# All transfers of a two-layer transformer kernel in the order of emission, with stores a little behind what they store

## The chip, the cores and the metric

The kernel runs on one core of one Trainium2 chip. The metric is the device time of one execution in microseconds. Before the change it is 3485.12 us, the median of three runs (3480.47, 3485.12 and 3489.89).

A core has engines with an instruction queue each: TensorE (PE, matrix products), VectorE (DVE), ScalarE (ACT), GpSimd (POOL) and SyncE (SP). In this kernel SP does nothing but issue transfers, and it issues all of them.

## What is computed

A transformer with two layers works on 1024 latent tokens (a grid of 16 x 64) and 256 context tokens, 1024 features each, all in fp32. Layer 0 mixes tokens with neighbourhood attention (16 heads, a window of 8 x 16, a bias by relative position, and the whole context), layer 1 with grouped-query attention (16 query heads, 4 key heads, root-mean-square norm of queries and keys, rotary positions). A SwiGLU FFN (hidden size 2816) follows each mixer. Shift, scale and gate of every norm are modulations made from a condition vector by the weights `ada_w`. Cut from the reference:

```python
for i in range(2):
    mod_l = (silu(c) @ ada_w[i] + ada_b[i]);  mod_c = (silu(c_ctx) @ ada_w[i] + ada_b[i])
    sh1, sc1, g1, sh2, sc2, g2 = split(mod)          # for latents (l) and context (c) apart
    a_l, a_c = ada_norm(h, norm_mix[i], sh1_l, sc1_l), ada_norm(hc, norm_mix[i], sh1_c, sc1_c)
    y_l, y_c = neighbourhood_attention(...) if i == 0 else qknorm_gqa(...)
    h = h + g1_l * y_l
    h = h + g2_l * swiglu_ffn(ada_norm(h, norm_ffn[i], sh2_l, sc2_l), ffn_w_in[i], ffn_w_out[i])
    if i == 0: ...                                   # the same for hc
return rms_norm(h, norm_final)

# neighbourhood attention, of one query row
p = softmax(concat([q @ k_window * scale + bias (masked), q @ k_context * scale]))
o = p[..., :n] @ v_window + p[..., n:] @ v_context
```

## The kernel before

**Numbers.** Every product is made from three: each fp32 operand is split in a high and a low part, and the kernel adds high x high, high x low and low x high. So most tiles exist twice (`qh` and `ql`, `wh` and `wl`, `ah` and `al`).

**Stages.** A startup makes the first norm and the first projections. Then comes the attention of layer 0 in two passes over its query tiles. A unit is 128 queries of one head, a pair is two units. Pass A has 48 pairs (16 heads, three pairs each), pass B 32 (16 heads, two each). Pass A runs beside the projections of queries, keys and values of the heads that come later, pass B beside the output projection. Then the FFN of layer 0, the projections that layer 1 starts with, its attention (64 pairs), its FFN and the last norm.

**One pair.** Scores `S` and `X` from keys `K` and queries `Qs` (PE), bias and maximum (DVE), exponentials and sums `Pt` (ACT), `Pt` scaled by the reciprocal sum `rc` (POOL, L803), transposed by PE (`T`, L810), split into high and low (`pT`, ACT L818 and DVE L823), multiplied with the values (`o`, L492), copied by ACT (`ob`, L832), the high and low columns added by POOL (`r`, L838). Of two heads that share 128 features, the second one's pair gets a tile `z`: two transfers of 64 x 256 put rows of the one head's `r` and of the other's into it (`z<-r`; the rows 0-63 and 64-127 change places), POOL adds the rest (L850, L851), and a transfer stores it (`Od<-z` in layer 0, `O1d<-z` in layer 1).

**Through DRAM.** Queries and keys go to scratch in DRAM, from where each head loads `Qs`, `K` and `Vt`. A block's projection ends in `finish_qk0` (layer 0; ACT makes `qh` at L755, DVE `ql` at L757) or `finish_qk1` (layer 1), and `stack_out` stores `qh` and `ql` as two transfers of 2x64x512, 2x64x256 for the context block: `dst[:, 0:64, c0:c0 + n]` has the two heads of a pair as its first dimension. `finish_v0` stores values (`Vd<-vt`), `out_add0` the updated residual (`H0d<-xr`). The weights of the modulation are loaded in pieces `adaw` and summed on DVE (`adaj`, L487).

**What sets the order.** The stages of all pairs are issued by `Plan` in the order of a written-out table, which gives each stage a place within a period (`PERIODA = 7622`, `PERIODB = 5560`, `PERIOD1 = 8172` ns). Between them `Plan` opens slots for the background: `Lanes` (`bg`) holds the projections, weight splits, norms and modulation as generators and advances them by one instruction per slot of an engine. `bg.now` is the plan's clock: it counts table time (and 650 ns per `tick` outside of the table), not device time. `bg.sleep(ns)` makes a generator yield until the plan's clock has moved on; it puts no instruction anywhere.

From the attention of layer 0 to the end of the program one context sets which engines issue in the order of emission:

```python
top.enter_context(tc.manual_schedule(engines={ET.PE, ET.Activation, ET.DVE, ET.Pool}))
```

SP isn't in it, so the order of the transfers in SP's queue is chosen by the framework's scheduler when the program is built. On the chip SP takes them in that order. In the startup SP is in the set already.

Of the kernel before, what the change touches and what calls it, by code (L numbers as in the profile page):

```python
# [31 lines left out]
# columns of the packed vector array  # L32
# [40 lines left out]
def _build(tc, nc, I, O, top):  # L73
# [28 lines left out]
    silc = const.tile([P, 16], F32, name="silc")        # silu(c) | silu(c_ctx) as columns  # L102
# [33 lines left out]
    def norm(tag, src, there, n, tmp, bank, done, direct=0, line=0):  # L136
        """the reciprocal root mean square of a block, from its chunks as they come, then the steps done(rs); the squares
        of the last direct ones go to the tensor engine one by one"""
# [52 lines left out]
    def apply_norm(tag, src, rs, G, sh, ah, al, tmp):  # L191
        """the norm's gain and shift, split into hi and lo"""
# [21 lines left out]
    # DRAM scratch  # L214
# [23 lines left out]
    def exp_ln_tables(after):  # L238
        """the one table set that serves both Exp and Ln, once the last Silu is through"""
        with tc.issue_after(after.ins):  # L240
            s.preload_act_table_set("natural_log_exp_and_others")
# [3 lines left out]
    # ================= layer 0: modulation, first norm =================  # L245
    acts = [None] * 3

    # relative-position bias laid out per (head, query, key tile offset, key)
# [13 lines left out]
    def startup():  # L262
        """the norm of every block and the first projections, issued in the order of emission"""
        ET = mybir.EngineType
        with ExitStack() as ph:
# [69 lines left out]
            # silu(c) as rows on every partition  # L335
# [52 lines left out]
            def modulation(m):  # L388
                """shift on the vector engine, scale on the tensor engine"""
# [17 lines left out]
            def apply0(kc):  # L407
                """a chunk of the first block, already scaled by 1/rms"""
# [23 lines left out]
            def first_qk(b):  # L432
                """keys and queries of the first pair, chunk by chunk in turn"""
# [60 lines left out]
    class Ring:  # L494
        """places used in turn: one is free when what had it before was given back"""
# [18 lines left out]
    class Temps:  # L514
        """fixed tiles by name, each in use until it is given back"""
# [16 lines left out]
    class Job:  # L532
        """weight units and the generator of the products with them, which may start when the first need are there"""
# [5 lines left out]
    class Lanes:  # L539
        """work in the background of an attention, or on its own, for engines that issue in the order of emission: the  # L540
        products advance by cost, what comes before and after a group of them by one instruction per slot of its
        engine, and only when the step before it should be through"""
# [4 lines left out]
        def __init__(self, third):  # L547
            # weights: two places, and a third one as long as its pool is there
            self.third, self.wx = third, None
            self.rings = dict(w=Ring(3), x=Ring(2))  # L550
            self.lo, self.cap = "GD", 6.0       # engines of the weights' low parts, most credit
            self.main, self.credit, self.now = [], 0.0, 0.0
            self.lines = [], [], []             # by urgency
            self.busy = dict(A=0.0, D=0.0, G=0.0)   # until when an engine takes nothing
            self.enter("weights", self.weights(), 0.0, 1)
# [5 lines left out]
        def follow(self, job, gen):  # L561
            """later products with the same weights"""
            job.heir = self.add(job.tag, [], gen)
            return job.heir
# [15 lines left out]

        def sleep(self, ns):
# [4 lines left out]
        def slot(self, engine):  # L586
            for it in self.side:
# [10 lines left out]
        def place(self, kind):  # L598
            """a weight unit's tiles"""
# [10 lines left out]
        def weights(self):  # L610
            """the units of the next jobs in turn, each loaded and split into hi and lo"""
# [53 lines left out]
        def tick(self, cost=1.0):  # L665
            """a slot of every engine, outside the attention's table"""
# [74 lines left out]
    QCOL = (0, 768, 512)         # columns of the queries of each block: the first pass of the attention takes two  # L741
# [19 lines left out]
    # One attention unit is 128 queries of one head, a pair of them 256. Its stages are issued in the order of a  # L761
    # table that repeats for every pair, with slots between them for the background work.
# [5 lines left out]
    class Pair:  # L768
        """two units; the context's keys (part 0, of both units in one bank) and the other parts"""
        def __init__(self, h, b, wid, blocks):  # L770
            self.h, self.b, self.nm = h, b, None
# [62 lines left out]
        def r(self):  # L834
            """sum of the hi and lo columns; of the second head of two, the rows 0-63 and 64-127 change places"""
# [4 lines left out]
            if self.h % 2 == 1:  # L840
                self.z_ = pb.tile([P, 256], F32, name="z", bufs=2)
                self.r0, self.r1 = rr[0, self.b], r
                dma(out=self.z_[0:64, :], in_=self.r0[64:128, :])
                dma(out=self.z_[64:128, :], in_=self.r1[0:64, :])

        def z(self):
            """both rows summed into the two heads' 128 features"""
            if self.h % 2 == 1:
                z = self.z_
                g.tensor_tensor(z[0:64, :], z[0:64, :], self.r0[0:64, :], ALU.add)  # L850
                g.tensor_tensor(z[64:128, :], z[64:128, :], self.r1[64:128, :], ALU.add)  # L851
                dma(out=self.out[self.h // 2][:, self.b * P:(self.b + 2) * P], in_=z[:])
                self.written.add((self.h // 2, self.b))

    class Plan:
        """the stages of all pairs in the order of their tables"""
# [3 lines left out]
        def __init__(self, phases):  # L860
            """of each phase: period, table, pairs, background products per slot, time until the next"""
# [27 lines left out]
    class Halves:  # L889
        """a block's 8 chunks in two tiles"""  # L890
# [7 lines left out]
    class Ffn:  # L898
        """what is left of a layer's output projection, that of block 1, and the FFN. The norms of the other blocks run
        behind the projection, that of block 1 behind the first products of the others"""  # L900
        def __init__(self, layer, blks, last, resid, g1, g2):
# [15 lines left out]
            if layer == 0:  # L917
                bg.add(tag, out(NJ - 4), lambda job: self.mm2(job, NJ - 4, whole), dst="x")
                # the last products of the context first
# [5 lines left out]
            # the last products of block 0 before those of block 1  # L925
# [14 lines left out]
        def start(self, h, tmp, hp, wx, psp, pool, norm):  # L940
            """with what the attention left; norm(b) gives gain and shift"""
# [70 lines left out]
        def silu(self, j, b, ps, k):  # L1012
# [6 lines left out]
            last = s.activation(sa[:, :n], ps[:, :n], AF.Silu)  # L1019
            self.rings["a"].give(k)  # L1020
            self.gates[j, b] = sa, i
            if (j, b) == (NJ - 1, 1):
                exp_ln_tables(last)
# [846 lines left out]
```

## Time and profile before

| what | us |
|---|---|
| median of three runs | 3485.12 |
| lowest and highest run | 3480.47, 3489.89 |
| span of the profiled execution | 3479.7 |
| PE busy | 3157.8 (91%) |
| DVE, ACT, POOL busy | 1951.5, 1362.9, 1008.5 |
| bytes moved | 363.41 MB, 194855 packets |

The profiled execution has no time of its own beside its span of 3479.7 us. The granted clock of PE over it is 0.957 of full speed. In the stages: the startup ends at about 170 us, pass A at about 790, pass B at about 990; the FFN of layer 0 goes to 2000, the preparation of layer 1 to 2100, its attention to 2690, and its FFN and the end to 3480.

In rows of the profile, L12 is a line of the kernel, `out<-in` names the tiles, and x is a count of instructions. In a view of waits a row reads: engine, instruction, what it waited for, us in total, times, the longest. SPq is SP's queue, with the time that each issue took. In a view of windows PE, PEld (weight loads), DVE, ACT and POOL have their busy time, then come the granted clock, the mean busy share of the 16 DMA engines and GB/s.

### The profile page before, as it was taken

To read this page: it belongs to the slowest core of one execution; us is meant where nothing else is said; L and a number is where in the kernel's file an instruction comes from. 1 tells how busy PE (TensorE), PEld (TensorE's weight loads), DVE (VectorE), ACT (ScalarE), POOL (GpSimd) and SP (SyncE) were. 2 spreads that over 40 slices of the span, in tenths; PEclk is the share of its full clock that TensorE was granted. 3 is DMA by queue.
4 is the path that set the end of the run, shared out by engine and by line. 5 is a ranking of instruction groups with operands and counts; after the bars stand their busy time and mean duration, and the time that the engine had idled before them with its cause. 6 is when DMAs were issued, how large, how long until landed. Compare 5 with 4: busy or idle time off the path is not lost.

```text
span 3479.7 us, 48144 instructions
## 1 busy us (share of the span) xinstructions
PE 3157.8 (91%) x17352; PEld 2706.9 (78%) x17352; DVE 1951.5 (56%) x4147; ACT 1362.9 (39%) x3305; POOL 1008.5 (29%) x959
## 2 busy tenths in 40 slices
PE   6767786868999999999999978999999999999998
PEld 4657685757877888888888767888888788888887
DVE  6347454556767655333333747898897534334335
ACT  3224342446753111111111437898887421121123
POOL 3224343445752000000000414666654200000002
PEclk8878898988999999999999989999999999999999
DMA  6546454556853343111111242333332211111111
GB/s 225 133 146 193 147 165 138 161 178 193 249 175 122 115 132 104 37 37 37 37 37 43 104 129 82 100 93 96 100 100 72 88 55 49 43 55 49 43 55 61
DMA packets 194855, 363.41 MB, mean 104 GB/s; under 512 B 30393, under 2 KB 94265, under 8 KB 192569
## 3 DMA queue, kind: packets, MB, share of 16 engines
q1 hardware_dynamic: 194616, 360.33, 32.8%
q8 instruction: 138, 2.26, 0.3%
q14 instruction: 101, 0.82, 0.1%
HBM read 283.71 MB, written 70.64 MB: 102 GB/s over the span
## 4 chain that ended last, share of the span: by engine, by line
PE 60%; DVE 4%; DMA 3%; ACT 1%; POOL 1%; issue 1%; DVEq 0%; ACTq 0%; POOLq 0%; SPq 0%
PE pg L714 5%; PE pa L714 5%; PE pg L713 5%; PE pg L715 5%; PE pa L715 5%; PE pa L713 5%; PE pm L1056 5%; PE pm L1057 5%; PE pm L1055 5%; PE T L810 3%; PE o L492 3%; PE S L1543 1%; PE S L1544 1%; PE ps L713 1%; PE ps L715 1%; PE ps L714 1%
## 5 line engine op out<-in xcount | busy, mean ns | idle before, releaser
L634 POOL TENSOR_TENSOR wl<-wr,wh 128x512 fp32r<-128x512 f32 x119 | 158.6, 1334 | 1443.6 <-ACT wh L632 1436.0
L803 POOL TENSOR_SCALAR Pt<-Pt,rc 128x1280 f32<-128x1280 f32 (+3 forms) x288 | 298.4, 1036 | 495.7 <-DVE rc L798 208.1
L810 PE MATMUL T<-ident,Pt 128*128 128x128 f32 x1952 | 312.9, 281 | 141.2 <-POOL Pt L803 136.5
L818 ACT CAST pT<-T 128x256 fp32r<-128x256 f32 (+2 forms) x672 | 305.1, 477 | 234.9 <-PE T L810 230.7
L810 PEld LDWEIGHTS T<-ident,Pt 128*128 128x128 f32 x1952 | 241.9, 144 | 198.7 <-POOL Pt L803 148.6
L823 DVE TENSOR_TENSOR pT<-T,pT 128x256 fp32r<-128x256 f32 (+2 forms) x672 | 342.2, 535 | 43.1 <-ACT pT L818 42.6
L632 ACT CAST wh<-wr 128x512 fp32r<-128x512 f32 x334 | 207.7, 623 | 343.3 <-PE pg L714 158.6
L714 PE MATMUL pa<-al,wh 128*128 128x512 f32 (+1 forms) x880 | 325.3, 370 | 6.1 <-POOL al L132 4.8
L1055 PE MATMUL pm<-hh,woh 128*128 128x512 f32 (+1 forms) x912 | 330.4, 362 | 0.0
L1056 PE MATMUL pm<-hl,woh 128*128 128x512 f32 (+1 forms) x912 | 329.4, 361 | 0.0
L1057 PE MATMUL pm<-hh,wol 128*128 128x512 f32 (+1 forms) x912 | 329.3, 361 | 0.0
L1067 DVE SCALAR_TENSOR_TENSOR h<-pm,modB,h 128x512 f32<-128x512 f32 (+1 forms) x368 | 242.4, 662 | 150.3 <-PE pm L1057 150.3
L1019 ACT ACTIVATE sa<-pa 128x512 f32<-128x512 f32 (+1 forms) x110 | 60.9, 554 | 676.6 <-PE pa L715 676.5
L713 PE MATMUL ps<-ah,wh 128*128 128x512 f32 (+1 forms) x688 | 273.4, 397 | 57.7 <-DVE ql L757 20.2
L713 PE MATMUL pa<-ah,wh 128*128 128x512 f32 (+1 forms) x880 | 324.2, 368 | 1.2 <-ACT ah L197 1.2
L713 PE MATMUL pg<-ah,wh 128*128 128x512 f32 (+1 forms) x880 | 325.1, 369 | 0.0
L715 PE MATMUL pa<-ah,wl 128*128 128x512 f32 (+1 forms) x880 | 324.5, 369 | 0.1
L714 PE MATMUL pg<-al,wh 128*128 128x512 f32 (+1 forms) x880 | 324.2, 368 | 0.0
L715 PE MATMUL pg<-ah,wl 128*128 128x512 f32 (+1 forms) x880 | 323.7, 368 | 0.0
L492 PE MATMUL o<-pT,Vt 128*128 128x256 f32 x1952 | 298.9, 292 | 9.6 <-DVE rc L797 8.6
L1031 DVE TENSOR_TENSOR sa<-sa,pg 128x512 f32<-128x512 f32 (+1 forms) x110 | 69.8, 634 | 392.1 <-PE pg L715 392.1
L634 DVE TENSOR_TENSOR wl<-wr,wh 128x512 fp32r<-128x512 f32 x215 | 170.2, 792 | 206.0 <-ACT wh L632 205.7
(260 smaller groups left out, 7397.5 us busy)
## 6 DMA issues: line engine op xcount, KB each, us to landing
wr<-in_fin SPq DMA_DIRECT2D x88, 512.0 KB
adaw<-in_adaT SPq DMA_DIRECT2D x160, 256.0 KB
wr<-in_wqkv SPq DMA_DIRECT2D x53, 512.0 KB
wr<-in_fout SPq DMA_DIRECT2D x44, 512.0 KB
wr<-in_wo SPq DMA_DIRECT2D x32, 512.0 KB
z<-r SPq DMA_DIRECT2D x144, 64.0 KB
aw<-in_ada0n SPq DMA_DIRECT2D x8, 1024.0 KB
Qs<-Q1d SPq DMA_DIRECT2D x32, 256.0 KB
```

The lines of the kernel that those rows point to most:

```text
L492: t.matmul(o_ap, lhsT=u.V[:, kb, :], rhs=u.pT[:, i, :], start=i == 0, stop=i == len(u.blocks) - 1)
L634: (g if self.engine == "G" else v).tensor_tensor(lo[:, c], raw[:, c], hi[:, c].bitcast(F32), ALU.subtract)
L713: t.matmul(ps, lhsT=hi[:, c], rhs=ah[:, kc, :n], start=kc == 0, stop=False)
L714: t.matmul(ps, lhsT=hi[:, c], rhs=al[:, kc, :n], start=False, stop=False)
L715: t.matmul(ps, lhsT=lo[:, c], rhs=ah[:, kc, :n], start=False, stop=kc == KC - 1)
L803: g.tensor_scalar(Pt, Pt, u.rc[:, 2:3], 1.0, ALU.mult, ALU.mult)
L810: t.transpose(T[:, i * P:(i + 1) * P], u.Pt[:, (i0 + i) * P:(i0 + i + 1) * P], ident[:])
L818: s.copy(u.pT[:, i0:i0 + n, :P], u.T[c])
L823: v.tensor_tensor(u.pT[:, i0:i0 + n, P:], u.T[c], u.pT[:, i0:i0 + n, :P].bitcast(F32), ALU.subtract)
L1055: t.matmul(ps[:, :n], lhsT=hi[:, c], rhs=hh[:, cols], start=i == 0, stop=False)
L1056: t.matmul(ps[:, :n], lhsT=hi[:, c], rhs=hl[:, cols], start=False, stop=False)
L1057: t.matmul(ps[:, :n], lhsT=lo[:, c], rhs=hh[:, cols], start=False, stop=i == 1)
```

## The change

SP joins the engines that issue in the order of emission, and some stores and exchanges are emitted later by the plan's clock than what makes them. For this `Lanes` gets a list of calls that are due at a time of the plan's clock: `later` enters one, and every slot first makes those that are due. Comments and docstrings are removed, which is not shown.

```diff
-        top.enter_context(tc.manual_schedule(engines={ET.PE, ET.Activation, ET.DVE, ET.Pool}))
+        top.enter_context(tc.manual_schedule(engines={ET.PE, ET.Activation, ET.DVE, ET.Pool, ET.SP}))
...
     class Lanes:
+        count = itertools.count()
...
+            self.due = []
...
+        def later(self, ns, fn):
+            heapq.heappush(self.due, (self.now + ns, next(self.count), fn))
+
+        def flush(self, end=None):
+            while self.due and (end is None or self.due[0][0] <= end):
+                heapq.heappop(self.due)[2]()
...
         def slot(self, engine):
+            self.flush(self.now)
...
     class Pair:
         def r(self):
...
                 self.r0, self.r1 = rr[0, self.b], r
+                bg.later(1600, self.swap)
+
+        def swap(self):
+            if not self.swapped:
+                self.swapped = True
                 dma(out=self.z_[0:64, :], in_=self.r0[64:128, :])
                 dma(out=self.z_[64:128, :], in_=self.r1[0:64, :])
+
+        def store(self):
+            dma(out=self.out[self.h // 2][:, self.b * P:(self.b + 2) * P], in_=self.z_[:])
+            self.written.add((self.h // 2, self.b))
 
         def z(self):
             if self.h % 2 == 1:
+                self.swap()
                 z = self.z_
                 g.tensor_tensor(z[0:64, :], z[0:64, :], self.r0[0:64, :], ALU.add)
                 g.tensor_tensor(z[64:128, :], z[64:128, :], self.r1[64:128, :], ALU.add)
-                dma(out=self.out[self.h // 2][:, self.b * P:(self.b + 2) * P], in_=z[:])
-                self.written.add((self.h // 2, self.b))
+                bg.later(2200, self.store)
...
         def finish_qk0(ps, dst, scale, b):
...
             banks["free"] += 1
+            yield from bg.sleep(1300)
             stack_out(dst, hi[:, :n], lo[:, :n], BLK[b][0] if scale is None else QCOL[b], n)
...
         # finish_v0 and out_add0, ahead of their stores
+            yield from bg.sleep(1300)
...
     # finish_qk1
-        tp.give(xn, qh, ql)
+        tp.give(xn)
+        yield from bg.sleep(1300)
         stack_out(dst, hi[:, :n], lo[:, :n], c0, n)
+        tp.give(qh, ql)
...
     # at the last Silu of an FFN: the next table set is loaded without a tie to that instruction
-                exp_ln_tables(last)
+                exp_ln_tables(None)
```

The listings below are rows of SP's queue, in its order: first the program before, then the changed one. The number in a name tells the instances of a tile apart; an instance may have another number in the other program.

The first place is in pass A, near its beginning, where the queries of the third pair of heads are stored (`Qd2_94<-qh`, `ql`) and weights of the modulation are loaded. Before:

```order
L81 DMA adaw_1505<-in_adaT0 128x512
L81 DMA Qd2_94<-qh_1540 2x64x512
L81 DMA Vt_1647<-Vd0_108 128x640
L81 DMA wr_1558<-in_wqkv0 128x1024
L81 DMA Qd2_94<-ql_1541 2x64x512
L81 DMA Qd2_94<-qh_1600 2x64x256
L81 DMA Vt_1647<-Vd0_108 128x256
L81 DMA braw_1650<-Bd_91 128x384
L81 DMA Qd2_94<-ql_1601 2x64x256
L81 DMA adaw_1531<-in_adaT0 128x512
```

And now:

```order
L81 DMA adaw_1505<-in_adaT0 128x512
L81 DMA adaw_1531<-in_adaT0 128x512
L81 DMA wr_1558<-in_wqkv0 128x1024
L81 DMA Qd2_94<-qh_1540 2x64x512
L81 DMA Qd2_94<-ql_1541 2x64x512
L81 DMA adaw_1619<-in_adaT0 128x512
L81 DMA Qd2_94<-qh_1600 2x64x256
L81 DMA Qd2_94<-ql_1601 2x64x256
L81 DMA Vt_1647<-Vd0_108 128x640
L81 DMA Vt_1647<-Vd0_108 128x256
L81 DMA braw_1650<-Bd_91 128x384
```

Stores of `qh` and `ql` stand directly behind each other, the two `adaw` loads that stood on both sides of these stores stand ahead of them, and the loads of the values (`Vt_1647`) come behind them all.

The second place is also in pass A, at the exchanges of `z_3379` and `z_3482` and the stores of the keys `Kd4_104`. Before:

```order
L81 DMA z_3379<-r_3377 64x256
L81 DMA Kd4_104<-qh_3396 2x64x512
L81 DMA wr_3412<-in_wqkv0 128x1024
L81 DMA Od2_114<-z_3379 128x256
L81 DMA Kd4_104<-ql_3397 2x64x512
L81 DMA Qs_3632<-Qd3_95 128x768
L81 DMA z_3621<-r_3268 64x256
L81 DMA K1_3633<-Kd3_103 128x640
L81 DMA z_3482<-r_3480 64x256
L81 DMA adaw_3588<-in_adaT0 128x512
L81 DMA K2_3634<-Kd3_103 64x640
L81 DMA Kd4_104<-qh_3504 2x64x512
```

And now:

```order
L81 DMA z_3379<-r_3035 64x256
L81 DMA z_3379<-r_3377 64x256
L81 DMA wr_3412<-in_wqkv0 128x1024
L81 DMA Kd4_104<-qh_3394 2x64x512
L81 DMA Kd4_104<-ql_3395 2x64x512
L81 DMA Od2_114<-z_3379 128x256
L81 DMA adaw_3453<-in_adaT0 128x512
L81 DMA Vt_3488<-Vd1_109 128x640
L81 DMA Vt_3488<-Vd1_109 128x256
L81 DMA braw_3491<-Bd_91 128x384
L81 DMA z_3482<-r_3133 64x256
L81 DMA z_3482<-r_3480 64x256
```

The two halves of a `z` now stand together, the store `Od2_114<-z_3379` comes behind both key stores instead of between them, and the next head's loads (`Qs_3632`, `K1_3633`), which stood among these stores, come after this piece.

The third place is in the attention of layer 1, where the keys and values of the third of the four key heads are loaded (`K1`, `K2` and `Vt`, 128x1280 each in all). Before:

```order
L81 DMA o32_21356<-O1d0_136 128x512
L81 DMA K1_20436<-K1d1_134 128x1280
L81 DMA Qs_19664<-Q1d2_127 128x512
L81 DMA K2_20437<-K1d1_134 64x1280 x2
L81 DMA z_19863<-r_19604 64x256
L81 DMA Q1d3_128<-ph_19700 2x64x512
L81 DMA z_19726<-r_19724 64x256
L81 DMA Vt_20441<-V1d_135 128x1280
L81 DMA Q1d3_128<-pl_19701 2x64x512
L81 DMA O1d1_137<-z_19726 128x256
L81 DMA Qs_19930<-Q1d3_128 128x512
L81 DMA z_19863<-r_19861 64x256
```

And now:

```order
L81 DMA z_20259<-r_20257 64x256
L81 DMA wr_20318<-in_wqkv1 128x1024
L81 DMA O1d2_138<-z_20259 128x256
L81 DMA z_20388<-r_20134 64x256
L81 DMA z_20388<-r_20386 64x256
L81 DMA K1_20450<-K1d1_134 128x1280
L81 DMA K2_20451<-K1d1_134 64x1280 x2
L81 DMA Vt_20455<-V1d_135 128x1280
L81 DMA Qs_20457<-Q1d4_129 128x512
L81 DMA Q1d5_130<-ph_20359 2x64x512
L81 DMA Q1d5_130<-pl_20360 2x64x512
L81 DMA O1d2_138<-z_20388 128x256
```

The loads of the group were spread between exchanges and stores of a pair of heads (`z_19726`) that lies well ahead of the group's use; now they stand together, behind the exchange of `z_20388`, a pair that comes later in the program.

More of the change, by code (lines that the diff above doesn't have):

```diff
@@ L238, in exp_ln_tables @@
     def exp_ln_tables(after):
-        with tc.issue_after(after.ins):
+        with tc.issue_after(after.ins) if after else ExitStack():
             s.preload_act_table_set("natural_log_exp_and_others")
@@ L770, in __init__ @@
         def __init__(self, h, b, wid, blocks):
-            self.h, self.b, self.nm = h, b, None
+            self.h, self.b, self.nm, self.swapped = h, b, None, False
             self.u = [Unit(), Unit()]
@@ L1018, in silu @@
             sa = self.tmp.tile([P, 512], F32, name="sa", bufs=2)
-            last = s.activation(sa[:, :n], ps[:, :n], AF.Silu)
+            s.activation(sa[:, :n], ps[:, :n], AF.Silu)
             self.rings["a"].give(k)
@@ L1487, in finish_qk1 @@
         e.tensor_tensor(lo[:, :n], x[:, :n], hi[:, :n].bitcast(F32), ALU.subtract)
-        tp.give(xn, qh, ql)
+        tp.give(xn)
+        yield from bg.sleep(1300)
         stack_out(dst, hi[:, :n], lo[:, :n], c0, n)
+        tp.give(qh, ql)
     heads1 = {}
```

## The prediction

> **What bounds the kernel now.** First the span, then the busy time by stages (window in us; its length; busy time of each engine with its instructions; granted clock, DMA share, GB/s).
>
> ```profile
> span 3479.7 us, 48144 instructions
> ```
> ```profile
> 170.00:790.00 620.00, 447.67 (x2737) 403.79 (x2736) 328.69 (x942) 228.25 (x670) 231.96 (x262) 0.86 0.51 160
> 790.00:990.00 200.00, 181.91 (x1226) 165.16 (x1225) 140.59 (x484) 137.50 (x418) 134.79 (x157) 0.96 0.72 212
> 990.00:2000.00 1010.00, 993.33 (x5135) 849.26 (x5134) 503.14 (x871) 222.03 (x405) 147.47 (x115) 0.99 0.24 79
> 2000.00:2100.00 100.00, 77.67 (x396) 62.51 (x395) 47.16 (x87) 43.61 (x97) 17.55 (x13) 0.90 0.42 123
> 2100.00:2690.00 590.00, 571.53 (x3781) 499.93 (x3779) 506.05 (x1160) 497.57 (x1305) 350.36 (x312) 0.99 0.31 92
> 2690.00:3480.00 790.00, 773.06 (x3473) 639.18 (x3471) 338.42 (x473) 181.99 (x315) 72.99 (x55) 0.99 0.17 56
> ```
>
> The first number behind each length is PE. The two FFNs (rows three and six) are PE with 17 us idle each: nothing that transfers do is worth much there. The first pass of the layer-0 attention (170 to 790, "pass A") has 620 - 447.67 = 172 us without PE, more than half of what the kernel has, at a clock of 0.86. Pass B has 18, the preparation of layer 1 (2000 to 2100) 22, its attention 18. Whatever this change does is decided in pass A. Its waits (who waits for whom; us, times, longest):
>
> ```profile
> POOL z L851 <- DMA z<-r: 119.3, 20, 20.3
> DVE adaj L487 <- DMA adaw<-in_adaT: 75.3, 12, 17.0
> PE T L810 <- POOL Pt L803: 133.4, 30, 16.2
> DVE ql L757 <- DMA Kd<-ql: 25.6, 6, 9.7
> DVE ql L757 <- DMA Qd<-ql: 25.6, 4, 11.0
> PE ps L713 <- DVE ql L757: 20.2, 5, 8.5
> ```
>
> PE waits for the scaled probabilities Pt; POOL, which makes them, stands in order behind a z that waits for its halves to be exchanged, and DVE, which makes their scale, behind an adaj that waits for weights. So the roots are transfers, and these are issued by SP alone. What SP's queue waits for in the same window, the two largest:
>
> ```profile
> SPq L81 <- POOL z L851: 58.7, 18, 8.4
> SPq L81 <- DMA Kd<-ql: 48.3, 15, 4.8
> ```
>
> One such place, by the timelines of SP and POOL and a window:
>
> ```profile
> 263.54 0.56 SPq L81 DMA_DIRECT2D Kd<-qh  x1
> 272.62 0.33 SPq L81 DMA_DIRECT2D Od<-z  x1
> 273.05 0.49 SPq L81 DMA_DIRECT2D Kd<-ql  x1
> ```
> ```profile
> 271.62 0.98 POOL L851 TENSOR_TENSOR z<-z,r 64x256 f32<-64x256 f32 x1 [10.03 <-DMA z<-r]
> ```
> ```profile
> 265.00:275.00 10.00, 1.13 (x6) 1.13 (x7) 3.57 (x7) 0.35 (x2) 3.29 (x3) 0.55 0.21 65
> ```
>
> The store Od<-z is the next in SP's order and waits nine us for POOL's z, with a ready Kd<-ql and loads behind it, while PE does 1.13 us of work in ten and the transfers run at a share of 0.21. That is the loss the change can give back.
>
> **What order can't give back.** The stores of queries and keys (2x64x512) are narrow. A stretch in which they run alone, one of wide loads in the startup, the count of what pass A moves, and two issues:
>
> ```profile
> 170.00:174.00 4.00, 4.00 (x20) 3.30 (x19) 0.00 (x0) 0.60 (x1) 0.00 (x0) 1.00 0.13 51
> 10.00:20.00 10.00, 6.47 (x43) 3.91 (x42) 8.74 (x17) 5.63 (x12) 2.53 (x2) 0.84 1.00 416
> ```
> ```profile
> q1 hardware_dynamic: 61334, 98.86, 50.3%
> Kd<-qh SPq DMA_DIRECT2D x14, 256.0 KB
> Kd<-ql SPq DMA_DIRECT2D x14, 256.0 KB
> Qd<-qh SPq DMA_DIRECT2D x11, 256.0 KB
> Qd<-ql SPq DMA_DIRECT2D x11, 256.0 KB
> Qd<-ql SPq DMA_DIRECT2D x7, 128.0 KB
> Kd<-qh SPq DMA_DIRECT2D x7, 128.0 KB
> Kd<-ql SPq DMA_DIRECT2D x7, 128.0 KB
> Qd<-qh SPq DMA_DIRECT2D x6, 128.0 KB
> ```
> ```profile
> 164.53 4.74 SPq L81 DMA_DIRECT2D Qd<-qh  x1
> 169.37 4.95 SPq L81 DMA_DIRECT2D Qd<-ql  x1
> ```
>
> A share of 0.13 is two engines of sixteen, at 51 GB/s; 256 KB (0.262 MB) take 5.1 us, and SP's own issues back up behind them at the same pace (4.74 and 4.95 us instead of half a us). Pass A has 50 of 256 KB and 27 of 128 KB, 16.6 MB, or 326 us. The other 98.86 - 16.6 = 82.2 MB at 416 GB/s would take 198 us, in which these two engines carry their part too. Together 524 us, so of pass A's 620 at most 96 can go by any order of the same transfers. The Trainium skill, in "DMA: Bandwidth & Descriptors", section "Rules for kernel authors", has the same: an outermost dimension below 16 confines a transfer to that many engines. The rows agree (0.13 for two), and by that rule alone nothing is gained here: rival (a).
>
> **The change part by part.** No instruction is removed or added that costs time: the same DMAs are issued by the same queue, and the delays are of the plan's clock, which only picks the place in the order. The listing has two POOL instructions less and two DVE ones more (about a us each, by the row of z above), which is below any term. What moves:
>
> Pass A, stores and exchanges behind what makes them. Od<-z now comes 2200 ns of the plan later, so SP should no longer stand for POOL's z, 58.7 us in 18 waits. At the place above the transfers had almost drained; where narrow stores are still draining, SP's wait costs nothing. Half, -29. Both halves of z now stand together behind r; by the listing of the transfers, of the 24 exchanges 12 had narrow stores among the six transfers ahead of the second half, and now 4 have: that eases the 119.3 us of POOL, but the queue's bound is the same, so it is in that half. The weights adaw move up by 6 to 18 places to where they are emitted. DVE's longest wait for them, 17.0, and PE's longest for Pt, 16.2, are of one size; I take one of these as gone, -15, since the other eleven are in the same queue.
>
> Against it: qh and ql now leave together. By the listing, of 82 narrow stores of layer 0 28 stood directly behind another, now 45. A load behind a pair lands after 10.3 us instead of 5.1, unless it was early enough. Two such on PE's path, +10. The 1300 ns also hold the tiles qh and ql longer; DVE waits for these 51.2 us in 10 waits already, of which PE feels 20.2. Each longer by 1.3 x (620 of the trace against 48 pairs x 7.622 = 366 of the plan) = 2.2 us, 22 in all, of which PE feels 20.2/51.2: +9. Pass A: -29 - 15 + 10 + 9 = **-25**. Bounds: -96 by the engines' work; above, if each of the 17 new pairs is felt, 17 x 5.1 = 87, with the 9 and less the 44 saved: +52.
>
> Pass B and the loads of a head. These were hoisted by the scheduler and now leave where they are emitted.
>
> ```profile
> PE S L1270 <- DMA K<-Kd: 6.5, 8, 2.0
> PE S L1269 <- DMA K<-Kd: 4.4, 1, 4.4
> ```
>
> They are already just in time: 10.9 us of PE over 16 heads. By the plan, the last K stands 8.6 us ahead of its use instead of 10.4; 1.8 us at each head would be +29. But the loads no longer wait behind stores that wait for z, which would give back up to the 10.9. I take **+3**, near the row of 10.9, as the queue runs at 0.72 and has room.
>
> Layer 1, preparation. These links of the chain of waits are stores that the next load needs:
>
> ```profile
> 2059.87 11.25 DMA K1d<-ph
> 2071.84 17.63 DMA K1d<-ph
> ```
>
> Each of some four stores in a row leaves 1.3 us later, +5; the stores of h (2 MB, 5 us at 416 GB/s) now stand among those of V1d; the second group's loads, hoisted into this stretch, leave it, -5 or so. **+3**, between -10 and +15.
>
> Layer 1, attention. Keys and values of a group come 12.5 us of the plan ahead of use instead of 68.
>
> ```profile
> L81 SPq DMA_DIRECT2D K<-K1d x18: 320/468/1693, 2167.8 to 2531.1; - x18
> ```
>
> Three issues a group, so six groups. K1, K2 and Vt of a group are 1.97 MB, at pass B's 212 GB/s 9.3 us: hidden by 3 us, and not if a narrow pair (10.3) is ahead. **+1**, from -8 (its PE idle is 18) to 6 x (9.3 + 10.3 - 12.5) = +43. FFNs, startup, tail: the same order or PE-bound, 0.
>
> Sum -25 + 3 + 3 + 1 = -18 on the profiled 3479.7, 3461.7. The median run, 3485.1, lies 5.4 above that execution, so **3467 us**, 0.5% faster.
>
> **Rivals.** (a) Pass A is bound by its narrow stores, and order moves the wait from z and adaw to whatever is behind them. For it: 326 us on two engines, and PE's clock and idle time don't depend on which wait is named. Against: the share of 0.21 at 265 to 275. Gains of 20 against +9, +10 and +7: within 5 us of 3485. (b) The loads' head start is what hid the narrow stores. A load that is hoisted past a qh and ql pair lands in time; in order of emission it stands behind it. It decides from the point where 10.3 us exceed the lead: pass B's 8.6 is below that, layer 1's 12.5 just above. 16 heads x 1.8 = +29, and half of the layer-1 bound, +21, less 25 give +25: 3510; with pass A's gain gone as well 3535. The skill's section "Queues, rings and completion order" in the same page has each engine take descriptors in the order of its ring, which is what makes a load wait there; the 4.74 us issue agrees. (c) The stalls on POOL and DVE go altogether. Pairs finish at
>
> ```profile
> L832 ACT COPY ob<-o x48: 579/587/592, 208.7 to 772.6; 128x512 f32<-128x512 f32 x48
> L832 ACT COPY ob<-o x6: 586/587/592, 285.0 to 326.7; 128x512 f32<-128x512 f32 x6
> ```
>
> 12.0 us each over pass A (563.9 / 47), and 8.3 in a quiet stretch (41.7 / 5), where there are few narrow stores. At that pace 47 x 3.7 = 172 would go; the two engines stop it at 96: 3485 - 70 to 3485 - 96, about 3400. (d) The scheduler's order was near that of emission, and nothing changes: not so in pass A, where the listing of SP differs in most rows, but true of the FFNs.
>
> **Chances.** My forecast 0.45 (3450 to 3476), (a) and (d) 0.22, (b) 0.22, (c) 0.11. 0.3% is 10.5 us, about the spread of the three runs (3480.47 to 3489.89), and what can be told from no change. Faster by over that: 0.43 of the forecast's and (c)'s 0.11, with 0.01 of (a): 0.55. Within: the rest of (a) and (d) and 0.01 of the forecast, 0.22. Slower: (b) and 0.01 of the forecast, 0.23. The range leaves out half of (b) and half of (c): 3410 to 3510. The forecast's own range is 3450 to 3476.
>
> **What would show it.** Right: in pass A SP's wait for POOL z near nothing, POOL's for z<-r below 80, DVE's for adaw below 60, PE busy 447 in about 595 instead of 620, the last ob copy at about 750. The waits for Kd<-ql and Qd<-ql on DVE grow to some 70. Pass B: PE's wait for K 10 to 20. Layer 1: no wait of PE for K<-K1d over 3 us. (a) shows the same PE idle with other names on it, (b) PE waiting for K in pass B with 2 us at each head or Vt and K at the groups, (c) pairs at 8 to 9 us throughout. I am wrong if the two-engine time isn't a floor, that is if pass A ends before 690, or if it ends later than 795.

## The result, and the profile after

The changed kernel takes 3602.72 us (median of four runs, 3599.16 to 3605.32) against 3486.1 for the kernel before in the same session: 1.0336 of it, with a 95% interval of 1.032 to 1.0353. It is 117 us slower. The forecast was 3467, and the top of the range 3510.

The span of the changed kernel, and three of its stages (length, busy PE, PEld, DVE, ACT, POOL, granted clock, DMA share, GB/s): pass A, pass B, the attention of layer 1.

```profile
span 3601.1 us, 48031 instructions
```
```profile
170.00:835.00 665.00, 449.04 (x2684) 404.60 (x2684) 316.17 (x916) 220.69 (x647) 212.28 (x248) 0.82 0.46 143
835.00:1067.00 232.00, 193.04 (x1244) 173.54 (x1243) 149.32 (x510) 144.68 (x440) 138.96 (x163) 0.91 0.67 198
2180.00:2800.00 620.00, 573.52 (x3763) 500.43 (x3762) 508.58 (x1162) 497.58 (x1308) 347.07 (x309) 0.98 0.30 88
```

In its window of pass A PE is busy about as long as before, but the window is 45 us longer, and everything beside PE is less used: the DMA share went from 0.51 to 0.46. Windows set by eye don't hold the same work, so the stages are best measured between ACT's copies `ob`, one for each pair of units: 48 in pass A, 32 in pass B, 64 in layer 1. From the starts of the first and the last copies (for pass B from pass A's last):

| stage, us | before | changed | difference |
|---|---|---|---|
| start to first copy | 208.7 | 210.0 | +1 |
| pass A, first to last copy | 563.9 | 625.0 | +61 |
| pass B | 210.0 | 231.8 | +22 |
| FFN of layer 0 and preparation of layer 1 | 1115.2 | 1113.3 | -2 |
| attention of layer 1 | 582.7 | 619.7 | +37 |
| last FFN and end | 799.3 | 801.2 | +2 |

Pass A between these copies, before and then changed:

```profile
208.70:772.60 563.90, 415.00 (x2572) 375.06 (x2571) 308.38 (x884) 214.30 (x629) 218.97 (x246) 0.87 0.51 162
210.00:835.00 625.00, 426.21 (x2573) 384.71 (x2572) 305.14 (x885) 214.72 (x629) 207.89 (x243) 0.83 0.47 146
```

PE has the same work in both, but for a product or two. Its busy time is 11 us longer, at a granted clock of 0.83 instead of 0.87, and the other 50 us are idle time (148.9 before, 198.8 now).

The waits of the engines in pass A, those that answer to the ones shown of before:

```profile
POOL z L871 <- DMA z<-r: 190.6, 20, 19.6
PE T L821 <- POOL Pt L814: 163.0, 25, 17.5
DVE adaj L487 <- DMA adaw<-in_adaT: 52.9, 11, 17.0
DVE ql L768 <- DMA Kd<-ql: 24.9, 7, 8.4
DVE ql L768 <- DMA Qd<-ql: 23.0, 3, 9.6
```

And SP's queue there:

```profile
SPq L81 <- DVE rawB L487: 89.7, 17, 10.9
SPq L81 <- POOL z L872: 30.7, 10, 4.2
SPq L81 <- DMA Kd<-ql: 28.4, 8, 4.6
```

SP's wait for POOL's z fell from 58.7 to 30.7, as the change has it. In its place stands one that was 19.5 before: SP waits 89.7 us for the products `adaj` of DVE (which write `rawB`), because the next load `adaw` goes into a tile that they still read. Behind it stands the exchange of z, and POOL's wait for it is 190.6 instead of 119.3. One such round, by the timelines of SP, POOL and PE:

```profile
305.54 0.33 SPq L81 DMA_DIRECT2D Od<-z  x1
305.96 9.72 SPq L81 DMA_DIRECT2D adaw<-in_adaT  x2
...
319.58 1.24 SPq L81 DMA_DIRECT2D z<-r  x2
```
```profile
323.20 0.71 POOL L871 TENSOR_TENSOR z<-z,r 64x256 f32<-64x256 f32 x1 [12.30 <-DMA z<-r]
```
```profile
325.35 0.69 PE L821 MATMUL T<-ident,Pt 128*128 128x128 f32 x2 [9.29 <-POOL Pt L814]
```

Two adaw loads take SP 9.7 us: the second waits for DVE. Then come the next head's loads, and then the exchange, for which POOL, and behind it PE, have been waiting. In pass B and in layer 1 SP can be seen to stand for another pair of transfers:

```profile
849.39 0.38 SPq L81 DMA_DIRECT2D Od<-z  x1
859.10 0.80 SPq L81 DMA_DIRECT2D o<-Od  x2
859.98 0.38 SPq L81 DMA_DIRECT2D Qs<-Qd  x1
860.41 1.62 SPq L81 DMA_DIRECT2D K<-Kd  x3
```
```profile
868.33 0.66 PE L1292 MATMUL S<-K,Qs 128*128 128x384 f32 x1 [9.13 <-DMA K<-Kd]
```
```profile
2463.31 6.37 SPq L81 DMA_DIRECT2D O1d<-z  x1
2478.29 0.33 SPq L81 DMA_DIRECT2D o<-O1d  x1
```
```profile
2481.91 0.62 ACT L1592 CAST ah<-o 128x512 fp32r<-128x512 f32 x1 [12.89 <-DMA o<-O1d]
```

The load `o<-Od` reads what the store `Od<-z` writes, and is now emitted right behind it. SP stands from one to the other, 9 us for a store of 128 KB with narrow ones ahead of it in the first case and 8.6 in the second, and K's loads, or ACT's next copies, are late by that. But SP's time at such places is hardly new. For `Od<-z` to land it waited 43.7 us over both passes before (150 to 1060 us) and 32.7 now, all but 0.2 of it in pass B:

```profile
SPq L81 <- DMA Od<-z: 32.5, 8, 10.2
```

For `O1d<-z` in the attention of layer 1 it was 15.2 before and is 22.4. New is what stands behind: PE's wait for K in pass B went from 10.9 to 30.1, ACT's for `o<-O1d` in layer 1 from 6.7 to 27.4. What grew most among SP's own waits in layer 1 is the one for DVE to be through with a weight tile (`wl`), from 46.1 to 124.4.

### The profile page after: what moved, and what is told of

It is laid out like the page before. It is cut to its first block, busy times and chain, and to the rows that moved or that the text cites. A ratio compares the mean times of both kernels' runs of the same rounds, so it can differ in the third digit from the quotient of the medians.

```text
span 3601.1 us, 48031 instructions
## 1 busy us (share of the span) xinstructions
PE 3186.1 (88%) x17352; PEld 2728.3 (76%) x17352; DVE 1950.3 (54%) x4149; ACT 1363.7 (38%) x3305; POOL 997.3 (28%) x957
## 4 chain that ended last, share of the span: by engine, by line
PE 57%; DVE 4%; DMA 3%; ACT 1%; POOL 1%; issue 1%; SPq 0%; DVEq 0%; ACTq 0%; POOLq 0%
PE pg L725 5%; PE pg L724 5%; PE pg L726 5%; PE pa L725 5%; PE pa L726 5%; PE pa L724 5%; PE pm L1076 5%; PE pm L1075 5%; PE pm L1077 5%; PE T L821 3%; PE o L492 3%; PE S L1568 1%; PE S L1569 1%; PE ps L724 1%; PE ps L725 1%; PE ps L726 1%
## 5 line engine op out<-in xcount | busy, mean ns | idle before, releaser
L492 PEld LDWEIGHTS o<-pT,Vt 128*128 128x128 f32 x1952 | 260.2, 193 | 33.3 <-DVE pT L834 18.0
```

Of the source, the lines that this page charges most:

```text
L492: t.matmul(o_ap, lhsT=u.V[:, kb, :], rhs=u.pT[:, i, :], start=i == 0, stop=i == len(u.blocks) - 1)
```

## The experiments

Each ratio is to the kernel before on the same chip. Stage times are from the copies, as in the table.

### The order, or the delays?

The change does two things, and each was done alone. The first run takes SP out of the manual order again; the second leaves SP in it and has none of the delays. Both load the table set behind the last Silu without a tie, as the change does; the first shows that this costs nothing.

```diff
 # first run: the changed kernel
-top.enter_context(tc.manual_schedule(engines={ET.PE, ET.Activation, ET.DVE, ET.Pool, ET.SP}))
+top.enter_context(tc.manual_schedule(engines={ET.PE, ET.Activation, ET.DVE, ET.Pool}))
 # second run: the kernel before
-top.enter_context(tc.manual_schedule(engines={ET.PE, ET.Activation, ET.DVE, ET.Pool}))
+top.enter_context(tc.manual_schedule(engines={ET.PE, ET.Activation, ET.DVE, ET.Pool, ET.SP}))
-                exp_ln_tables(last)
+                exp_ln_tables(None)
```

> The changed kernel with SP's queue again in the scheduler's order: only the delays (and the small moves on the engines that they bring) are left. Theory O (the order of SP's queue costs the 121 us: in order of emission SP stands for instructions that aren't through yet, and what is queued behind it is late): 3475 to 3500. Theory D (the delays cost it: every store and exchange leaves later, and the loads that need them too): 3570 to 3610.

> The kernel before with SP in the order of emission and no delay; PE, DVE, ACT and POOL have the same order as before, instruction by instruction (the one tie of the last table load is gone, as in the change). Theory O: slower than the change, since SP now also stands for each z and each qh right behind its emission: 3620 to 3700. Theory D: near 3485.

The delays alone: 3481.69 us, ratio 0.9991 (0.9981 to 1.0), pass A 564.7, pass B 209.9, layer 1 579.9. They cost nothing and gain next to nothing, as long as the scheduler places the transfers. The order alone: 3590.33, ratio 1.0302 (1.0285 to 1.0319), pass A 595.5, pass B 238.8, layer 1 621.5. Since the other engines' orders are the same there, row for row, the whole of these 107 us is SP's order. That it would be slower than the change with its delays was wrong: it is 12 us faster. The delays cost 30 us more in pass A once the order is that of emission, and give 7 back in pass B. With the order alone POOL's wait for z<-r in pass A is 119.4 us, as long as before, and SP's for the tiles of adaw is 83.2: the longer wait for the exchange goes with the delays, and the other 32 us of pass A are lost without it.

### The narrow stores

The prediction had the narrow stores as the floor of pass A. So they were made wide, in the kernel before and in the changed one: each half of `stack_out` becomes two transfers with 64 rows as their first dimension.

```diff
-        dma(out=dst[:, 0:64, c0:c0 + n], in_=tmp_hi)
-        dma(out=dst[:, 64:128, c0:c0 + n], in_=tmp_lo)
+        for r, x in ((0, tmp_hi), (64, tmp_lo)):
+            for i in range(2):
+                dma(out=dst[i, r:r + 64, c0:c0 + n], in_=x[i * 64:i * 64 + 64])
```

> The kernel before, each 2x64xn store of queries and keys split into two of 64xn, so that the outermost dimension has 64 rows; nothing else. Theory N (narrow stores on two engines are what makes pass A long): their 326 us go to about 40, and pass A's 620 us come down by 60 to 130; 3355 to 3430. Against it (the two engines are only busy while everything waits for something else): 3470 to 3490.

> The changed kernel with the same split of the stores. If the order of emission costs only because a late load stands behind a narrow pair (10.3 us), the cost of 117 us over the kernel before mostly goes: within 25 us of the run with the split alone. If it costs because SP stands in order for things that aren't ready, it stays: 70 to 120 us above that run.

The kernel before with wide stores: 3227.84 us, ratio 0.9264 (0.925 to 0.9278). That is 255 us, or 7.4%, far more than expected, and the fastest kernel of this study. The first copy comes at 157.4 instead of 208.7, pass A takes 403.1 instead of 563.9, pass B 190.2 instead of 210.0, layer 1 570.8 instead of 582.7. Its window of pass A, and four of its stores with their size and the median us to landing:

```profile
170.00:560.00 390.00, 368.22 (x2502) 334.59 (x2501) 308.75 (x854) 205.76 (x609) 219.64 (x243) 1.00 0.75 226
```
```profile
Kd<-qh SPq DMA_DIRECT2D x24, 128.0 KB, 3.7
Kd<-ql SPq DMA_DIRECT2D x24, 128.0 KB, 2.9
Qd<-qh SPq DMA_DIRECT2D x20, 128.0 KB, 2.8
Qd<-ql SPq DMA_DIRECT2D x20, 128.0 KB, 2.5
```

PE is busy 368 of 390 us at full clock, and the share is 0.75 where it was 0.51: the stores no longer have two engines to themselves while the others are idle.

The changed kernel with wide stores: 3360.95, ratio 0.9644 (0.9626 to 0.9661). It is 133 us behind the other, more than the 117 without. So narrow stores are not why the order of emission costs. Its pass A takes 499.2, 96 us more than the other's, and pass B 220.4, 30 more. The same two waits stand in it (SP's, and POOL's; from 165 to 760 us, so with the first part of pass B):

```profile
SPq L81 <- DVE rawB L487: 84.5, 18, 12.0
```
```profile
POOL z L872 <- DMA z<-r: 128.1, 22, 15.5
```

In the kernel before with wide stores these are 17.6 and 21.3. Only in layer 1 was part of the loss due to the narrow stores: it is 11 us there (581.6 against 570.8) instead of 37.

### Place by place

Now each place at which SP was seen to stand was moved in the changed kernel, one at a time: the adaw loads 4000 ns of the plan later, and their products with them; the loads of the heads' results only 5000 ns after their store; the exchange at once.

```diff
 # adaw: its load, as go(), no longer at its place
+                    clock.later(4000, go)
 # the results
-            self.written.add((self.h // 2, self.b))
+            bg.later(5000, lambda: self.written.add((self.h // 2, self.b)))
 # and out_add0 stores the residual without its sleep(1300)
 # the exchange
-                bg.later(1600, self.swap)
+                self.swap()
```

> The changed kernel, with each load of modulation weights (adaw) emitted 4000 ns of the plan after its place, so that DVE should be through with the tile's last contents when SP comes to it. Theory Q (in order of emission the head of SP's queue stands on a transfer that can't start, here a load into a tile that DVE still reads, and the exchange of z behind it comes late): SP's wait for DVE rawB in pass A falls from 90 us below 30, pass A from 625 (first to last of its 48 ob copies) to 575 to 600, the time to 3555 to 3580. Rival (SP waits there only because it is ahead of the others; the wait is harmless): 3590 to 3610, pass A 615 to 630.

> The changed kernel, with the loads of the heads' results (o<-Od, o<-O1d) allowed only 5000 ns of the plan after the store that they read, instead of right behind it; the store of the residual goes out without its delay, since it would otherwise stand behind a load that waits for it. Theory Q: SP no longer stands for Od<-z and O1d<-z to land; pass B from 232 to 210 to 222, the attention of layer 1 from 620 to 590 to 605, the time 3555 to 3580. Rival (pass B and layer 1 lose because keys and queries are emitted later, just ahead of use): unchanged, 3590 to 3610.

> The changed kernel with both halves of z exchanged right at the place of r instead of 1600 ns of the plan later. Order alone, with no delay, had 595 in pass A against the change's 625. If the exchange's delay makes this difference (it lets adaw loads and narrow stores get ahead of it), pass A is 590 to 605 and the time 3570 to 3585; if the delays of the stores make it, 3595 to 3610.

adaw later: 3575.29, ratio 1.0266 (1.0251 to 1.0281). Pass A is 596.0 instead of 625.0, within what was expected. SP's wait for the tiles is halved, not gone (below 30 was expected), and POOL's for z<-r falls from 190.6 to some 155:

```profile
SPq L81 <- DVE rawB L495: 45.5, 10, 10.4
```

Results later: 3580.12, ratio 1.0283 (1.0266 to 1.03). Layer 1's attention goes from 619.7 to 597.7, as expected, but not by the expected way: SP's wait there for `O1d<-z` to land stays (22.4 in the change, 21.6 here), while ACT's wait for the load falls from 27.4 to 14.0. Pass B doesn't get shorter (237.7), which was a miss, though SP's wait for `Od<-z` to land fell from 32.5 to 7.1 there. So that wait alone isn't what makes pass B long. The exchange at once: 3581.84, ratio 1.0286 (1.0271 to 1.0301), pass A 601.0: of the 30 us that the delays cost on top of the order in pass A, the exchange's own has 24. POOL's wait for z<-r is 112.1 instead of 190.6, and DVE's for adaw 89.4 instead of 52.9.

For pass B the keys were tried: the next head's loads one pair earlier.

```diff
-                    elif self.i == 1 and nxt[1] < 2:
+                    if self.i == 1 - ps and nxt[1] < 2:
                         load_head(*nxt)
+                    if self.i == 1 and nxt[1] < 2:
                         bg.enter("bias", bias(*nxt))
```

> The changed kernel, with the loads of the next head's queries and keys emitted one pair earlier in pass B (5.56 us of the plan more of lead). If pass B loses because these loads, in their emitted place, have too little lead for what SP stands on ahead of them: PE's wait for K in pass B from 30 us below 10, pass B from 232 to 212 to 220, the time 3580 to 3592. If something else holds pass B up: 228 to 234, no change.

3607.29, ratio 1.0362 (1.0344 to 1.038), and pass B 232.8: nothing. Yet PE's waits for K are gone. In pass B, of the change and then of this run:

```profile
PE S L1292 <- DMA K<-Kd: 22.5, 5, 9.1
POOL z L871 <- DMA z<-r: 11.0, 2, 8.1
PE S L1293 <- DMA K<-Kd: 7.6, 8, 1.4
```
```profile
POOL z L871 <- DMA z<-r: 36.9, 8, 11.0
PE S L1294 <- DMA K<-Kd: 4.6, 7, 1.5
PE S L1293 <- DMA K<-Kd: 1.4, 1, 1.4
```

The time that PE spent on K came back as POOL's wait for the exchange: 24 us less here, 26 more there. The exchange, moved forward, had gained 24 us in pass A; here a load moved forward only handed the wait on.

### Together

> The changed kernel with all four: adaw later, exchange at once, o later (and the residual's store without delay), keys of pass B a pair earlier; narrow stores as they are. If the four places are the whole of the loss: pass A 565 to 580, pass B 210 to 218, layer 1's attention 595 to 600, the time 3490 to 3520. If the single effects overlap or come back elsewhere: 3530 to 3560.

The four together: 3522.72, ratio 1.0119 (1.0103 to 1.0136). Pass A 586.6, pass B 215.8, layer 1 599.9. That is as forecast but for pass A, which was to be 580 or less, and it puts the time 3 us above the forecast's range. Pass B, which neither of its two places moved alone, has 16 of its 22 us back when both are moved with the exchange. Which of them it needs wasn't tried. For what is left of layer 1, two more places were moved: the loads of projection weights, and the split of the results on ACT.

```diff
-                        raw = wraw.tile([P, D], F32, name="wr")
-                        job.srcs[job.loaded](raw)
+                        self.later(3000, go)      # go() takes the tile and loads it; in layer 1's attention alone
...
-            ready = bg.now + 3000
+            ready = bg.now + 9000
```

> The run with all four and narrow stores, with two more places moved in the attention of layer 1 alone: each load of projection weights (wr) 3000 ns of the plan later, since SP stands 115 us there for DVE to be through with the tile, and the split of a head's results 9000 ns of the plan behind its load instead of 3000, since ACT still waits 17 us in 5 places for it. If these are what is left of layer 1's loss (its attention took 600 in that run, 583 before the change): 583 to 590, the time 3503 to 3515. If not: 598 to 602, 3520 to 3525. Layer 0 stays as it was.

3508.58, ratio 1.0076 (1.0059 to 1.0093), and layer 1's attention at 584.6, where the kernel before has 582.7. SP's wait there for DVE to be through with a weight tile, 124.4 in the change, is 53.7. Pass A still had 20 us too many. Two guesses were left: DVE's waits for adaw, which are longer now that its loads are later, and the 1300 ns ahead of the stores.

```diff
 # one run
-                    clock.later(4000, go)
+                    clock.later(3000, go)
-                    e[3] = clock.now + 4000    # when the products may follow
+                    e[3] = clock.now + 6500
 # the other, in finish_qk0 and finish_v0
-            yield from bg.sleep(1300)
```

> The last run with the adaw loads 3000 instead of 4000 ns of the plan late, and their products on DVE 6500 instead of 4000 ns behind the load. If DVE's waits for adaw (88 us in pass A there) hold up the remaining 20 us of pass A: those waits below 40, pass A 560 to 572, the time 3485 to 3500. If they are only where DVE happens to stand: pass A 580 to 588, 3505 to 3512.

> The run before (adaw 4000 and 4000) without the delay of 1300 ns ahead of the stores of layer 0's queries, keys and values. If that delay holds tiles that ACT and DVE wait for and so costs the remaining 20 us of pass A: pass A 563 to 573, 3488 to 3500. If not: 580 to 588, 3505 to 3512.

The first: 3515.01, ratio 1.009 (1.0065 to 1.0114), pass A 583.3; the time is even 3 us above what was expected without an effect. DVE's wait for adaw in the run before, and then in this one:

```profile
DVE adaj L495 <- DMA adaw<-in_adaT: 90.6, 18, 14.1
```
```profile
DVE adaj L495 <- DMA adaw<-in_adaT: 30.8, 11, 12.7
```

60 us of waiting are gone and nothing is gained, so that guess falls.

The second: 3485.97, ratio 1.0002 (0.999 to 1.0014). Pass A 563.8, pass B 209.3, layer 1 582.7, against 563.9, 210.0 and 582.7 before. DVE's waits for the tiles of the stores, in the run before (longer numbers) and in this one:

```profile
DVE ql L787 <- DMA Qd<-ql: 34.5, 6, 12.5
DVE ql L787 <- DMA Kd<-ql: 33.5, 7, 8.7
```
```profile
DVE ql L787 <- DMA Qd<-ql: 24.7, 5, 9.1
DVE ql L787 <- DMA Kd<-ql: 15.3, 4, 6.7
```

SP's wait for the tiles of adaw in pass A, 89.7 in the change and 19.5 before:

```profile
SPq L81 <- DVE rawB L495: 22.0, 10, 3.6
```

So with six places moved and the 1300 ns of layer 0 taken back, the order of emission is as fast as the scheduler's, stage by stage, and of the 117 us none is left. The single effects overlap, so the 117 can't be shared out among the places; and whether the same places would also speed up the scheduler's order wasn't run. Last, whether it is also as good when the stores are wide:

> The same with the split stores. If the four places are the whole of the loss: within 30 us of the kernel before with split stores (3228), 3220 to 3260. If in order of emission something more is lost that the scheduler's order hides: 3270 to 3300.

> The last run but one (all six places moved) with the split stores. If the places are all of what the order of emission costs: within 10 us of the kernel before with split stores (3228). If the narrow stores hid a rest of it (with four places moved and split stores it was 3260, 32 more): 3240 to 3260. Pass A, 403 in the kernel before with split stores, tells it: 400 to 408 or 412 to 422.

With two places moved (adaw and results later) and wide stores the time was 3298.34 (ratio 0.9471, 0.9455 to 0.9486): 63 of the 133 us are back, fewer than expected (3240 to 3290). With four places moved 3259.87 (ratio 0.9367, 0.9348 to 0.9386), with all six 3249.48 (0.9321, 0.9298 to 0.9344). It isn't: 22 us remain to the scheduler's order with wide stores, most of them in pass A (421.4 against 403.1) and 8 in layer 1. Without the 1300 ns pass A gained nothing here (421.3 with four places), where it gained 20 with narrow stores. With narrow stores this rest didn't show, since both orders end at 564. What holds it up wasn't searched further.

## Why the prediction was wrong, point by point

**The step that failed** is the first term of the sum, "Od<-z now comes 2200 ns of the plan later, so SP should no longer stand for POOL's z, 58.7 us in 18 waits ... Half, -29". The wait did shrink (to 30.7), but a wait of an in-order queue isn't a sum that one item can be taken from. The question to ask was what the queue would stand on next. The scheduler's order had not only delayed things: it had also kept the loads of adaw apart from the last reader of their tile. In order of emission SP stands 89.7 instead of 19.5 us for these tiles in pass A, and pass A is 61 us longer, not 25 shorter. It ends at 835, past the 795 that the prediction named as its sign of being wrong. That the order of SP's queue does this is shown by the run with the order alone; that SP's standing for transfers that can't start is the way is shown for pass A by the loads of adaw (29 us back when they come later), and for the rest only by what all the moved places give together.

**adaw, -15.** DVE's wait for adaw fell as forecast (75.3 to 52.9, "below 60"), but the reason given, that the loads "move up ... to where they are emitted", didn't do it: with the order alone they stand there too, and the wait is 84.2. It fell because the exchanges came later, and they paid for it: with the exchange at once it is 89.4, and POOL's wait for z<-r, which was to be below 80, is 112.1 instead of 190.6. So the right number here was luck.

**Narrow pairs, +10.** They are there, but with wide stores the order costs 133 us instead of 117: not the reason.

**Tiles held longer, +9.** In the changed kernel the waits did not grow (47.9 us against 51.2, not 70). When the six places are moved they are 68.0, and taking the 1300 ns away there (with that of the values) gives 20 us, twice the size, and brings them down to 40.0. With wide stores it gives nothing, as it should if tiles held by narrow stores are the way. That fits the term, but the stores also leave earlier without the 1300 ns, and this wasn't told apart. In the change itself it doesn't show.

**Pass B, +3,** was +22. "The loads no longer wait behind stores that wait for z" left out that they now stand behind whatever else SP waits for there: for POOL's z 41.6 us instead of 23.0, and as long as before for a store to land. The forecast's sign that would show rival (b), "PE waiting for K in pass B", was seen (30 us), and taking it away changed nothing. Pass B came back only with several places moved at once, so which of them it hung on stays open.

**Layer 1's preparation, +3,** came, with the FFN, as -2, inside its range of -10 to +15. **Layer 1's attention, +1,** was +37. The keys' shorter lead was looked at and is harmless, as argued; the loads of the results and of the weights behind it were not looked at; with them moved, after the places of layer 0, 35 of the 37 are back.

**The floor of pass A** wasn't contradicted: no order with narrow stores that was run went below 563.8. With wide ones pass A fell by 161 us, where the floor had left 96 to any order and rival (c) had put the pace of a quiet stretch at 172 less: the pace came (403.1 / 47 = 8.6 us for a pair, against 8.3). Two engines alone couldn't have carried the stores at that pace: by the prediction's working, the 14.9 MB of them and the other 76.5 MB that the run with wide stores moved between 150 and 560 us would have taken 477 us (an estimate, at 51 and 416 GB/s) instead of 410. The rule of the Trainium skill, "DMA: Bandwidth & Descriptors", section "Rules for kernel authors", is that an outermost dimension below 16 confines a transfer to at most that many engines. The runs agree: narrow stores alone had a share of 0.13, two of sixteen, and with 64 rows for 2 pass A passed the pace of two engines. The rule was read in the prediction as a rival to the change's gain, and was the larger finding.

**Rival (b)** had the right side and priced at 3510 to 3535 what came as 3603. Its mechanism, a load behind a narrow pair, isn't the one that decided: with wide stores the loss is still there. **Rival (a)** had the wait move on to what stands behind, and it did, but at a cost and not at none.

## What to carry to other kernels

Putting SP's queue in the order of emission cost this kernel 107 us. A transfer that had to wait there made what stood behind it late; the clearest case was a load into a tile that was still read. A wait at the head of such a queue isn't worth its length: the one that the forecast took away shrank by 28 us, and another grew by 70. Moving a victim forward helped in one place (the exchange, 24 us of pass A) and only handed the wait on in another (the keys of pass B). So list for each transfer what it waits for and how late that is, move those that wait, and measure by stages and with the places together, since here they acted together. And look at the share of a transfer that runs alone before looking at its order: two of sixteen engines in one layout cost 7.4% of this kernel, twice what the order did.

## What was not expected of the hardware

Splitting 256 KB stores of two rows into two of 64 rows took 255 us from 3483, when they were thought to hold pass A alone: 51 us of it came ahead of the first copy. PE's granted clock, 0.957 over the kernel before and 0.942 in the changed one, was 0.989 with wide stores; in pass A it went from 0.87 to 1.00. For the same products between the first and the last copy of pass A PE is then busy 379.7 us instead of 415.0:

```profile
157.40:560.50 403.10, 379.69 (x2571) 344.72 (x2570) 317.57 (x885) 213.03 (x628) 223.95 (x248) 1.00 0.75 225
```

So 35 of the 161 us that pass A lost came with the higher clock, and 125 are idle time of PE that is gone (148.9 to 23.4). The clock was highest where PE stood idle least; why, no run here shows.
